# Strassen forms at a different address residue, and the transposed rows as views of one slab, in a two-layer encoder kernel

## The chip, the cores and the metric

The kernel runs on one core of a Trainium2 chip. The metric is the device time of one execution in microseconds; lower is better. TensorE (PE) multiplies; its operands come from the on-chip memory SBUF, where every one of 128 partitions holds the same byte range of a tile, so that a tile has one start address in each partition. Every matmul instruction has two SBUF operands: a stationary one of 128 columns (the "weights", brought in by a weight load that the profile shows on its own row, PEld) and a moving one of up to 512 columns. VectorE (DVE), ScalarE (ACT) and GpSimd (POOL) prepare operands and empty the accumulators; SyncE (SP) issues the DMAs.

## The reference, cut to what matters

Two layers work on one sequence of 512 rows of 1024. Each layer has a mixer (token attention with 12 heads, and attention to 256 memory rows with 4 heads) and a gated feed-forward part with 2816 hidden columns:

```python
h = rms_norm(x, g_mix_pre[i])
proj = h @ w_in[i]
# q, k, v, qm from proj; tok = banded or global attention; mo = memory attention
o = jnp.concatenate([tok, mo], axis=-1) @ w_o[i]
x = x + rms_norm(o, g_mix_post[i])
h = rms_norm(x, g_ffn_pre[i])
gu = h @ w_gate_up[i]
f = (jax.nn.silu(gu[..., :D_FF]) * gu[..., D_FF:]) @ w_down[i]
x = x + rms_norm(f, g_ffn_post[i])
```

## The kernel before

**Numbers in two halves.** A float32 operand is split into a high and a low half of the type fp32r (`split`, lines 284 to 294: ACT writes the high half, DVE the rest). A product is then three matmuls: high by high, high by low, low by high (`mm3`, lines 277 to 281).

**Seven products instead of eight.** In the feed-forward part the 512 tokens are cut into two halves of 256 and the gate and up columns are taken as two halves too; for 20 of the 22 column blocks of a layer a Strassen scheme computes the product by seven products of sums. The sums of the activations are the *forms*: `A11` and `A12` (tile `a1`), `A22` (`a22`), and `nS1`, `S2`, `S3`, `S4` (tile `sf`), each with a high and a low half. They are the moving operands. The sums of the weights (`whi`, `wlo`, tags `hi` and `lo` of the pool `whl`) are the stationary operands. One product is `seven` (lines 1035 to 1043): for each of 4 contraction blocks, three matmuls of 256 columns. One block `f` is thus 7 x 4 x 3 = 84 such matmuls; `body` (from line 1061) runs six of its own products and those of the next block between them, and the preparation of the following weights runs on ACT and DVE beside it. The 20 blocks of a layer go in three lots (6, 6 and 8 blocks), and after each lot the down projection follows (`down`, `down_prod`, 512 moving columns). The first two of the 22 blocks go the plain way (`plain`), with 256 moving columns out of `a1`, `a22` and `a21`.

**Transposed rows.** `hT` holds the transposed, normed rows for the q, k and v products; there it is the stationary operand, and weights of 256 or 384 columns move past it. `th` holds the transposed attention output for the product with `w_o`; it is stationary too, and 512 columns of weights move. In each layer `hT`, `th` and `sf` take turns in the same four places: the pool `hp` has four tiles `h00`, `h01`, `h10`, `h11` of 4 x 512 numbers (8192 bytes in each partition), and a new tile of the same tag waits until every reader of the old one is done.

**Order.** The order of PE's instructions is written out by hand (`manual_schedule`, and the lists of `mixer`); the other engines' order is the tile framework's. A wait is made where an instruction reads or writes a range that an earlier one wrote or read.

**Addresses.** The allocator hands out the tiles of a pool one behind the other; pools of the left side go upward, pools of the right side downward from the top. Nearly all sizes are multiples of 256 bytes, so that the table below gives the remainder of a start address modulo 256, which is what the change moves. Each k-block starts 1024 or 2048 bytes behind the last, so that all parts of a tile share its remainder. In the program before:

| operand | role | layer 0 | layer 1 |
|---|---|---|---|
| `whi`, `wlo` | stationary for forms, moving elsewhere | 192 | 192 |
| `a1`, `a22`, `a21` | moving | 224 | 224 |
| `sf` | moving | 192 | 224 |
| `hT`, `th` | stationary | 192 | 224 |

Of the kernel before, what the change touches and what calls it, by code (L numbers as in the profile page):

```python
# [9 lines left out]
F32 = mybir.dt.float32  # L10
F32R = mybir.dt.float32r
# [5 lines left out]
P = 128  # L17
S = 512
NT = S // P
D = 1024  # L20
KD = D // P
# [17 lines left out]
         (1, 3, LH), (0, 2, HL), (1, 2, HL), (0, 3, HL), (1, 3, HL))  # L39
LATE = {2: 1.2, ("r", 0): 1.05, ("r", 1): 1.3, 3: 2.2, ("r", 2): 2.4, ("r", 3): 3.4, ("m", 0): 4.5, ("m", 1): 5,  # L40
        "rows": 4, ("rm", 0): 6, ("rm", 1): 6.2}
LOTS = ((0, 8), (8, 14), (14, 22))

PACE = [{'lag': 1.692, 'vlag': 0.479, 'jstep': 0.213, 'kstep': 0.375, 'klag': 0.742, 'qoff': [0.212, 0.126, 0.099], 'qlag': 1.02, 'late': 0.6, 'moff': -0.235, 'mdur': 0.562, 'mlag': 0.697, 'kw': [0, 0, 0, 0], 'mw': [2, 1, 1, 0], 'qw': [0, 0, 0, 1, 3, 3, 3, 3], 'hoff': 0, 'ow': [10.3, 10.8, 12.2, 13.2], 'ox': 11.4, 'od': 0.3, 'hstep': 0.872, 'hlag': 1.742, 'hjstep': 0.135, 'hvlag': 0.751, 'owm': [0, 0, 0, 0, 0, 0, 0, 0], 'q0step': 0.27, 'q0off': -0.032, 'q0lag': 0.919, 'm0off': -0.078, 'm0dur': 0.002, 'm0lead': 1.887, 'mlead': 1.201, 'qlead': 0.921, 'q0lead': 1.555, 'qstep': 1.002, 'tw': [0, 0, 0, 0, 0, 0, 0, 0], 'h2off': 0}, {'lag': 1.824, 'vlag': 0.535, 'jstep': 0.218, 'kstep': 0.777, 'klag': 1.715, 'qoff': [-0.027, -0.162, -0.027], 'qlag': 1.189, 'late': 2.15, 'moff': -0.088, 'mdur': 0.384, 'mlag': 1.205, 'kw': [0, 0, 0, 0], 'mw': [0, 0, 0, 0], 'qw': [0, 0, 0, 0, 0, 3, 1, 1], 'hoff': 0, 'ow': [10.2, 10.7, 12.2, 13.2], 'ox': 11.3, 'od': 0.3, 'hstep': 0.946, 'hlag': 1.847, 'hjstep': 0.295, 'hvlag': 0.568, 'owm': [0, 0, 0, 0, 0, 0, 0, 0], 'q0step': 0.718, 'q0off': -0.018, 'q0lag': 1.136, 'm0off': -1.059, 'm0dur': 0.171, 'm0lead': 2.465, 'mlead': 3.162, 'qlead': 1.895, 'q0lead': 1.42, 'qstep': 0.998, 'tw': [0, 0, 0, 0, 0, 0, 0, 0], 'h2off': 0.016}]
# [76 lines left out]
    return bass.AP(tensor=ap.tensor, offset=ap.offset, ap=[[0, P], [1, n]])  # L121


class Forms:

    def __init__(self, trunk, keep, tmp, hp):
        self.tr, self.nc = trunk, trunk.nc
        two = lambda pool, k, tag: [pool.tile([P, k, 256], F32R, tag=f"{tag}{z}", name=tag, bufs=1) for z in range(2)]  # L130
        self.a1, self.a22, self.a21 = two(keep, KD, "a1"), two(keep, 4, "a22"), two(tmp, 4, "a21")
        self.as1 = tmp.tile([P, KD, 256], F32, tag="as1", name="as1", bufs=1)
        self.tmp, self.hp, self.s, self.left = tmp, hp, None, []

    def new_s(self):
        sf = [[self.hp.tile([P, 4, S], F32R, tag=f"h{q}{z}", name="sf", bufs=1) for z in range(2)] for q in range(2)]
        self.s = {n: [sf[i // 2][z][:, :, i % 2 * 256:i % 2 * 256 + 256] for z in range(2)]
                  for i, n in enumerate(("nS1", "S2", "S3", "S4"))}

# [49 lines left out]
class Trunk:  # L189
# [3 lines left out]

    def pool(self, stack, name, side="left", **kw):
        return stack.enter_context(self.tc.tile_pool(name=name, bufs=1, side=side, reuse_waits="tile", **kw))

    def psum(self, stack, name):
        return stack.enter_context(self.tc.tile_pool(name=name, bufs=1, space=bass.MemoryType.PSUM,
                                                      reuse_waits="tile"))
# [169 lines left out]
        return self.tagged(("acc", "acc", "s", "s", "s", "pv")[(self.nbank - 1) % 6])  # L369

    def new_hT(self):
        self.hT = [[self.hp.tile([P, 4, S], F32R, tag=f"h{q}{z}", name="hT", bufs=1) for q in range(2)]
                   for z in range(2)]
        return self.hT

# [428 lines left out]
    def heads_out(self, l, put, xw, xs, x0, dx):  # L804

        self.nbank = 0
        self.wo, self.po, self.th = {}, [], {}
        for u in range(4):
            self.unit(self.a["wo"][l, 0, u], self.side(l, "owm", u), put=put, x=xw[u], dst=self.wo, key=u,
                      pair=("wo", l, 0, u))  # L810

        def part(k):
            if k % 4 == 0:
                self.th[k // 4] = [self.hp.tile([P, 4, S], F32R, tag=f"h{k // 4}{z}", name="th", bufs=1)
                                   for z in range(2)]
            self.split(self.th[k // 4][0][:, k % 4], self.th[k // 4][1][:, k % 4], self.tok[:, k],
                       self.side(l, "tw", k))

        def prod(k, t):
            if t == len(self.po):  # L820
                self.po.append(self.bank())
                if t == 2:
                    self.held = self.turns.pop()
            self.prod(self.po[t], self.heads, KD, k, t, self.wo[k // 2])

        for k in range(KD):
            put(max(xs[k], x0 + (NFILL * k - 1.5) * dx) if k < NH // 2 else xs[k], lambda k=k: part(k))
        for k in range(NH // 2):
            for t in range(NFILL):
                put(max(x0 + (NFILL * k + t) * dx, xs[k] + 0.001 * (t + 1)), lambda k=k, t=t: prod(k, t))  # L830
# [136 lines left out]
    def ffn(self, l, pools, forms, late, done):  # L967
# [156 lines left out]

        for c, (f0, f1) in enumerate(LOTS):
            fs = list(range(f0, f1))
# [22 lines left out]
            for i, f in enumerate(gs):  # L1149
                more = gs[i + 1:] + [None, None]  # L1150
                body(f, f - f0, more[0], more[1], [first, second])
            if c < len(LOTS) - 1:
                self.down(get, self.a["wd"][l], fs, c, o, head)
# [115 lines left out]
    def run(self):  # L1269
        tc, nc, a = self.tc, self.nc, self.a  # L1270
        with ExitStack() as top:
            top.enter_context(tc.manual_schedule(engines={mybir.EngineType.PE}))
            glob = self.glob = self.pool(top, "glob")
            self.small = self.pool(top, "small")
            self.wraw = self.pool(top, "wraw")
            self.whl = self.pool(top, "whl")
            self.ps, self.nbank, self.turns = self.psum(top, "ps"), 0, ["s0", "s1", "s2"]
            dram = self.dram = top.enter_context(tc.tile_pool(name="dram", bufs=1, space=bass.MemoryType.DRAM))
            xs = [[dram.tile([P, D], F32, name=f"x{i}{t}", tag=f"x{i}{t}") for t in range(NT)] for i in range(3)]
            self.spill = dram.tile([P, 2, KD, NMEM], F32, name="smem", tag="smem")  # L1280
            x0 = [a["x"][0, t * P:(t + 1) * P] for t in range(NT)]
            out = [a["out"][0, t * P:(t + 1) * P] for t in range(NT)]

            cst = self.cst = glob.tile([P, 2 * P], F32, name="cst")
            self.ident = cst[:, :P]
            self.ropet = cst[:, P:2 * P].rearrange("p (a t d) -> p a t d", a=2, d=16)
            self.gcol = glob.tile([P, 2, KD], F32, name="gcol")
            self.sink, self.nsink = [glob.tile([P, NH], F32, name=z) for z in ("sink", "nsink")]
            self.gt = glob.tile([P, 2, 2, NT, HD], F32, name="gt")
            self.identr = glob.tile([P, P], F32R, name="identr")  # L1290
            self.mhalf = glob.tile([P, 4], F32, name="mhalf")
            nc.gpsimd.memset(self.mhalf, -0.5)

            hs = [ExitStack() for _ in range(DEPTH + 1)]
            self.hp = self.pool(hs[0], "hT0")
            hb, norm = ExitStack(), ExitStack()
            self.hbuf = self.pool(hb, "h0", side="right")
            self.norm_pool(norm)
            late = {}
            for l in range(DEPTH):  # L1300
                last = l == DEPTH - 1
                mix = ExitStack()
                tokp = self.pool(mix, f"tok{l}")
                core = ExitStack()
                mkp = self.pool(core, f"mk{l}")
                self.mT = tokp.tile([P, 2, KD, NMEM], F32R, tag="tok", name="mT", bufs=1)
                if l == 0:
                    late = self.start(mkp)
                norm.close()
                self.core = self.pool(core, f"core{l}")  # L1310
                self.more = self.core if l else None
                self.mixer(l, mkp, late, tokp)
                self.more = None
                core.close()
                hb.close()

                keep, fts, norm = ExitStack(), ExitStack(), ExitStack()
                forms = Forms(self, self.pool(keep, f"keep{l}", side="right"),
                              self.pool(fts, f"forms{l}", side="right"), self.hp)
                self.norm_pool(norm)  # L1320
                self.hT = None
                late = self.mix_out(l, forms, x0 if l == 0 else xs[1], xs[2 * l])
                mix.close()
                if not last:
                    self.todo = [("wq", 1, c, z) for c in (2, 3) for z in range(2)] + [("wo", 1, 0, u) for u in range(4)]
                ff = ExitStack()
                pools = dict(ff=ff, gu=self.pool(ff, f"gu{l}"), norm=norm, forms=fts)
                get, fs, o, head = self.ffn(l, pools, forms, late, keep.close)
                norm = ExitStack()
                if not last:  # L1330
                    self.hp = self.pool(hs[l + 1], f"hT{l + 1}", side="right")
                    hb = ExitStack()
                    self.hbuf = self.pool(hb, f"h{l + 1}", side="right")
                self.norm_pool(norm)
                late = self.ffn_out(get, a["wd"][l], fs, o, head, a["g_ffn_post"][l], a["g_mix_pre"][1], xs[2 * l], out if last else xs[1], None if last else self.new_rs())
                ff.close()
                if l == 0:
                    hs[0].close()
            norm.close()
            for z in hs[:0:-1]:  # L1340
                z.close()
# [30 lines left out]
```

## Time and profile before

| what | us |
|---|---|
| median of 3 runs (1107.42 to 1108.26) | 1107.56 |
| the profiled execution | 1108.23 |
| its span, first to last instruction | 1106.4 |
| the six runs of `seven` between down projections, 3144 of its 3360 matmuls | 370.4 |
| the rest of the matmul stream and what lies between | 736.0 |

The six runs lie at 221.25 to 276.92, 324.81 to 380.49 and 417.50 to 493.18 us in layer 0, and at 782.85 to 837.45, 885.64 to 940.24 and 977.15 to 1051.35 us in layer 1. Their sum is 55.67 + 55.68 + 75.68 + 54.60 + 54.60 + 74.20. A matmul's row in the timeline has a start that is recorded and an end that is modelled: matmuls follow each other faster than their rows are long. So a matmul's price in a stream is the distance from one start to the next, and where a window holds nothing but matmuls, its length over their number. A window also counts the instruction that began before it and is still open, so that 469 in its row mean 468 starts.

### The profile page before, as it was taken

What the parts mean: (1) busy time and instruction counts of PE and PEld (TensorE: products, weight loads), DVE (VectorE), ACT (ScalarE), POOL (GpSimd) and SP (SyncE); (2) the same over time, 40 slices, a digit from 0 to 9 for tenths busy, and PEclk for the clock granted to TensorE, in tenths of its full rate; (3) what the DMA queues carried; (4) which work ended last, traced back from release to release, by engine and by line L of the source; (5) the groups of instructions that cost most, each with busy time, mean ns of one, the idle gap of its engine ahead of it and who ended that gap; (6) DMA issues with size and microseconds to landing.
All of it is one profiled execution on the core that took longest, in us unless ns stands there. A gap on an engine that the chain in (4) does not pass through costs nothing.

```text
span 1106.4 us, 19515 instructions
## 1 busy us (share of the span) xinstructions
PE 1088.8 (98%) x7436; PEld 1000.2 (90%) x7436; DVE 842.2 (76%) x1433; ACT 659.3 (60%) x1357; POOL 194.9 (18%) x341
## 2 busy tenths in 40 slices
PE   9999999999999999999999999999999999999997
PEld 7899888999889989998898888879998899899986
DVE  7889876999458677875888988758995478668854
ACT  7679975865435535553567888747664365346531
POOL 5773231102000000000444542312000000000001
PEclk9999999999999999999999999999999999999999
DMA  9621017354832562335533221154236133422253
GB/s 335 248 78 39 20 35 252 116 165 133 303 124 86 180 221 78 113 101 190 195 124 115 77 77 39 39 189 154 72 106 207 55 100 115 129 76 97 83 165 115
DMA packets 40702, 142.44 MB, mean 129 GB/s; under 512 B 4768, under 2 KB 5152, under 8 KB 40480
## 3 DMA queue, kind: packets, MB, share of 16 engines
q1 hardware_dynamic: 40320, 140.80, 37.7%
q8 instruction: 58, 0.95, 0.4%
q10 hardware_dynamic: 288, 0.40, 0.1%
q14 instruction: 36, 0.29, 0.1%
HBM read 122.30 MB, written 18.87 MB: 128 GB/s over the span
## 4 chain that ended last, share of the span: by engine, by line
PE 84%; DVE 6%; ACT 4%; POOL 2%; DMA 2%; issue 1%; DVEq 0%; SPq 0%; POOLq 0%; ACTq 0%
PE ps L280 13%; PE ps L279 13%; PE ps L281 13%; PE ps L1043 12%; PE ps L1042 12%; PE ps L1041 12%; PE tp L644 3%; PE o L659 2%; PE o L658 2%; PE s L583 1%; PE s L584 1%; DVE mT L307 1%; ACT whi L289 1%; DVE tl L293 1%; DMA row<-in_x_dram 1%
## 5 line engine op out<-in xcount | busy, mean ns | idle before, releaser
L289 ACT ACTIVATE whi<-raw 128x1024 fp32r<-128x1024 f32 (+3 forms) x206 | 169.2, 839 | 175.9 <-PE ps L1043 73.5
L293 DVE TENSOR_TENSOR wlo<-raw,whi 128x1024 fp32r<-128x1024 f32 (+3 forms) x202 | 191.2, 961 | 74.5 <-ACT whi L289 71.3
L1042 PE MATMUL ps<-sf,wlo 128*128 128x256 f32 x640 | 179.7, 281 | 0.0
L1041 PE MATMUL ps<-sf,whi 128*128 128x256 f32 x640 | 179.7, 281 | 0.0
L1043 PE MATMUL ps<-sf,whi 128*128 128x256 f32 x640 | 179.7, 281 | 0.0
L280 PE MATMUL ps<-wlo,f 128*128 128x512 f32 (+1 forms) x360 | 138.6, 385 | 0.1
L279 PE MATMUL ps<-whi,f 128*128 128x512 f32 (+1 forms) x360 | 138.7, 385 | 0.0
L281 PE MATMUL ps<-whi,f 128*128 128x512 f32 (+1 forms) x360 | 138.4, 384 | 0.0
L1043 PE MATMUL ps<-a,whi 128*128 128x256 f32 x480 | 134.4, 280 | 0.0
L1041 PE MATMUL ps<-a,whi 128*128 128x256 f32 x480 | 134.3, 280 | 0.0
L1042 PE MATMUL ps<-a,wlo 128*128 128x256 f32 x480 | 133.8, 279 | 0.0
L1042 PEld LDWEIGHTS ps<-sf,wlo 128*128 128x128 f32 x640 | 121.4, 190 | 0.5
L1041 PEld LDWEIGHTS ps<-sf,whi 128*128 128x128 f32 x640 | 121.1, 189 | 0.5
L1043 PEld LDWEIGHTS ps<-sf,whi 128*128 128x128 f32 x640 | 121.4, 190 | 0.0
L322 POOL TENSOR_SCALAR e<-sso 128x1 f32<-128x1 f32 x8 | 3.4, 423 | 564.1 <-ACT junk L317 564.0
L634 POOL TENSOR_SCALAR p<-p,rd 128x256 f32<-128x256 f32 (+2 forms) x128 | 76.7, 618 | 101.4 <-DVE rd L631 46.2
L279 PE MATMUL ps<-whi,hT 128*128 128x256 f32 (+1 forms) x304 | 92.6, 305 | 0.0
L1042 PEld LDWEIGHTS ps<-a,wlo 128*128 128x128 f32 x480 | 90.5, 188 | 0.2
L1041 PEld LDWEIGHTS ps<-a,whi 128*128 128x128 f32 x480 | 90.4, 188 | 0.2
L1043 PEld LDWEIGHTS ps<-a,whi 128*128 128x128 f32 x480 | 90.1, 188 | 0.0
L280 PE MATMUL ps<-wlo,hT 128*128 128x256 f32 (+1 forms) x304 | 88.5, 291 | 1.3 <-DVE wlo L293 1.3
L281 PE MATMUL ps<-whi,hT 128*128 128x256 f32 (+1 forms) x304 | 88.2, 290 | 0.0
(207 smaller groups left out, 2703.9 us busy)
## 6 DMA issues: line engine op xcount, KB each, us to landing
raw<-in_wgu_dram SPq DMA_DIRECT2D x48, 512.0 KB, 4.5
raw<-in_wd_dram SPq DMA_DIRECT2D x44, 512.0 KB, 4.4
rb<-in_wgu_dram SPq DMA_DIRECT2D x40, 512.0 KB, 3.6
raw<-in_wo_dram SPq DMA_DIRECT2D x17, 512.0 KB, 4.1
raw<-in_wq_dram SPq DMA_DIRECT2D x16, 512.0 KB, 5.0
xt<-x SPq DMA_DIRECT2D x12, 512.0 KB, 5.2
raw<-in_wm_dram SPq DMA_DIRECT2D x8, 512.0 KB, 4.5
x<-y SPq DMA_DIRECT2D x8, 512.0 KB, 3.1
```

The lines of the kernel that those rows point to most:

```text
L279: mm(out, lh, rh, start=first, stop=False)
L280: mm(out, lh, rl, start=False, stop=False)
L281: mm(out, ll, rh, start=False, stop=last)
L289: a = nc.scalar.activation(hi, src, AF.Copy)
L293: b = nc.vector.tensor_sub(lo, src, hi.bitcast(F32))
L634: self.pooled = nc.gpsimd.tensor_scalar(hd["p"][z][:, :n], hd["p"][z][:, :n], rd[:, z:z + 1], 1.0, op0=OP.mult, op1=OP.mult)
L644: nc.tensor.transpose(tp[:, z], hd["p"][i][:, jj * P:(jj + 1) * P], self.ident)
L658: nc.tensor.matmul(o[:, c0:c1], hd["v"](j), th, start=(j == 0), stop=False, skip_group_check=True)
L659: nc.tensor.matmul(o[:, c0:c1], hd["v"](j), tl, start=False, stop=last, skip_group_check=True)
L1041: mm(out, wh[:, s], rh, start=start and k == 0, stop=False, skip_group_check=True)
L1042: mm(out, wl[:, s], rh, start=False, stop=False, skip_group_check=True)
L1043: mm(out, wh[:, s], rl, start=False, stop=k == 3, skip_group_check=True)
```

## The change

`hp` with its four tiles is replaced by one tile per layer (`hrows`, made by `slab`), and `hT`, `th` and `sf` become views of it at offsets of their own (`rows`; the offsets are in numbers of 4 bytes, in `PLACE`). The forms `a1` and `a22` become views of one tile, `a21` of another, 12 numbers (48 bytes) behind its start (`carve`, `FORM`). Two empty tiles (`gap`) of 224 and 32 bytes move the pools of the right side. No instruction is added or removed in the text of the kernel: splits, matmuls and transfers are the same, with other addresses.

The remainders modulo 256 that follow: in layer 0 the slab starts where `hp` did (192), so `th` (0 numbers) stays at 192, `hT` (22 numbers, 88 bytes) lies at 24 and `sf` (28 numbers, 112 bytes) at 48; the right side starts 224 bytes lower, which is at 0, and `a1`, `a22`, `a21` lie at 48. In layer 1 the gap of 32 bytes and the slab's 48 extra numbers put its start at 0, so `hT` (24 bytes) lies at 24, `th` (192 bytes) at 192, `sf` (48 bytes) at 48, and the forms below it at 48. The weights stay at 192.

| operand | layer 0 before, after | layer 1 before, after |
|---|---|---|
| `a1`, `a22`, `a21` | 224, 48 | 224, 48 |
| `sf` | 192, 48 | 224, 48 |
| `hT` | 192, 24 | 224, 24 |
| `th` | 192, 192 | 224, 192 |

```diff
+FORM = 12
+PLACE = (128, dict(hT=22, th=0, sf=28)), (48, dict(hT=6, th=48, sf=FORM))
...
+def carve(pool, name, ks):
+
+    t = pool.tile([P, 256 * sum(ks) + 64], F32R, tag=name, name=name, bufs=1)
+    cut = [(FORM + 256 * sum(ks[:i]), 256 * k) for i, k in enumerate(ks)]
+    v = [t[:, a:a + n].rearrange("p (k n) -> p k n", n=256) for a, n in cut]
+    return [v[i:i + 2] for i in range(0, len(v), 2)]
...
-        two = lambda pool, k, tag: [pool.tile([P, k, 256], F32R, tag=f"{tag}{z}", name=tag, bufs=1) for z in range(2)]
-        self.a1, self.a22, self.a21 = two(keep, KD, "a1"), two(keep, 4, "a22"), two(tmp, 4, "a21")
+        self.a1, self.a22 = carve(keep, "a1", [KD, KD, 4, 4])
+        (self.a21,) = carve(tmp, "a21", [4, 4])
...
-        sf = [[self.hp.tile([P, 4, S], F32R, tag=f"h{q}{z}", name="sf", bufs=1) for z in range(2)] for q in range(2)]
+        sf = [[self.tr.rows(q, z, "sf") for z in range(2)] for q in range(2)]
...
+    def gap(self, stack, name, n):
+
+        self.pool(stack, name, side="right").tile([P, n], F32, name="gap", bufs=1)
+
+    def slab(self, stack, l, **kw):
+
+        room, self.place = PLACE[l]
+        self.hrows = self.pool(stack, f"hT{l}", **kw).tile([P, 16 * S + room], F32R, name="hrows", bufs=1)
+
+    def rows(self, q, z, name):
+
+        a = self.place[name] + (2 * q + z) * 4 * S
+        return self.hrows[:, a:a + 4 * S].rearrange("p (k n) -> p k n", n=S)
...
-        self.hT = [[self.hp.tile([P, 4, S], F32R, tag=f"h{q}{z}", name="hT", bufs=1) for q in range(2)]
+        self.hT = [[self.rows(q, z, "hT") for q in range(2)]
                    for z in range(2)]
...
-                self.th[k // 4] = [self.hp.tile([P, 4, S], F32R, tag=f"h{k // 4}{z}", name="th", bufs=1)
+                self.th[k // 4] = [self.rows(k // 4, z, "th")
                                    for z in range(2)]
...
-            self.hp = self.pool(hs[0], "hT0")
+            self.slab(hs[0], 0)
...
+                if l == 0:
+                    self.gap(keep, "gap0", 56)
                 forms = Forms(self, self.pool(keep, f"keep{l}", side="right"),
-                              self.pool(fts, f"forms{l}", side="right"), self.hp)
+                              self.pool(fts, f"forms{l}", side="right"))
...
-                    self.hp = self.pool(hs[l + 1], f"hT{l + 1}", side="right")
+                    self.gap(hs[l + 1], "gap1", 8)
+                    self.slab(hs[l + 1], 1, side="right")
```

## What was predicted

> **What bounds the kernel now.** I read the page first, then PE's waits, then the matmul stream stage by stage, because the change touches nothing but addresses and can act on time only through instructions that read or write the moved tiles.
>
> ```profile
> span 1106.4 us, 19515 instructions
> PE 1088.8 (98%) x7436; PEld 1000.2 (90%) x7436; DVE 842.2 (76%) x1433; ACT 659.3 (60%) x1357; POOL 194.9 (18%) x341
> PEclk9999999999999999999999999999999999999999
> PE 84%; DVE 6%; ACT 4%; POOL 2%; DMA 2%; issue 1%; DVEq 0%; SPq 0%; POOLq 0%; ACTq 0%
> L1041 PE MATMUL ps<-sf,whi 128*128 128x256 f32 x640 | 179.7, 281 | 0.0
> L1041 PE MATMUL ps<-a,whi 128*128 128x256 f32 x480 | 134.3, 280 | 0.0
> ...
> PE tp L644 <- DVE tl L293: 2.6, 7, 0.7
> PE o L658 <- DVE tok L667: 2.4, 5, 0.7
> ```
>
> PE holds 84% of the chain that ended last, at the full clock in every slice, and its longest waits sum to a few microseconds in the whole span. Lines 1041, 1042 and 1043 each have 640 + 480 = 1120 instructions, so the forms' products are 3360 matmuls. Nothing before them was idle (the last column is 0.0), so their time is not waiting; it is the distance from one start to the next. The windows that hold only them show it:
>
> ```profile
> 324.81:380.49 55.68, 55.68 (x469) 1.00 0.32 107
> 417.50:493.18 75.68, 75.68 (x637) 1.00 0.30 96
> 885.64:940.24 54.60, 54.60 (x469) 1.00 0.33 108
> 977.15:1051.35 74.20, 74.20 (x637) 1.00 0.30 97
> ```
>
> Layer 0: 55.68/468 = 119.0 ns and 75.68/636 = 119.0 ns. Layer 1: 54.60/468 = 116.67 and 74.20/636 = 116.67. The same instructions, shapes and clock, and no wait: 2.3 ns differ. What differs in the code's terms is the form's remainder minus the weight's, modulo 256, which I call the offset. In layer 0 `sf` stands at offset 192 - 192 = 0 and the `a` forms at 32; in layer 1 all stand at 32. One product on `sf` (12 matmuls) in each layer, first and next start:
>
> ```profile
> 441.74 0.28 PE L1041 MATMUL ps<-sf,whi 128*128 128x256 f32 x1
> 441.86 0.28 PE L1042 MATMUL ps<-sf,wlo 128*128 128x256 f32 x1
> ...
> 443.18 0.28 PE L1041 MATMUL ps<-a,whi 128*128 128x256 f32 x1
> ...
> 999.90 0.28 PE L1041 MATMUL ps<-sf,whi 128*128 128x256 f32 x1
> 1000.02 0.28 PE L1042 MATMUL ps<-sf,wlo 128*128 128x256 f32 x1
> ...
> 1001.30 0.28 PE L1041 MATMUL ps<-sf,whi 128*128 128x256 f32 x1
> ```
>
> 1.44/12 = 120.0 ns at offset 0, 1.40/12 = 116.67 at 32. So PE's stream bounds the kernel, and the address has a price in it already. How much of a matmul is not streaming? Other streams without waits answer it:
>
> ```profile
> 22.87:24.78 1.91, 1.91 (x13) 1.00 1.02 392
> 27.03:29.67 2.64, 2.64 (x24) 1.00 0.77 271
> 163.28:189.17 25.89, 25.89 (x115) 1.00 0.76 263
> 569.79:573.00 3.21, 3.21 (x29) 1.00 0.50 158
> 724.31:750.90 26.59, 26.59 (x115) 1.00 0.62 219
> ```
>
> These have `hT` or `th` as stationary operand. Each count is one or two above the starts in the window. At offset 0 (layer 0): 384 columns 1.91/11 = 173.6 ns, 256 columns 2.64/22 = 120.0, 512 columns 25.89/114 = 227.1. From 256 to 512 columns that is 107.1/256 = 0.418 ns a column; 256 columns stream in 107 ns, and a **remainder** of 13 ns is left, the same at every length. At offset 32 it is 116.67 - 107 = 9.7. At offset 224, that is -32 (layer 1): 3.21/27 = 118.9, remainder 11.9; 26.59/114 = 233.2, remainder 19.2.
>
> **The change part by part.**
>
> *Forms to offset 112.* After the change every form lies at 48, the weights at 192: 48 - 192 = -144, or 112. No row of this trace has that offset, nor any start at an odd multiple of 16, so its remainder is bounded by the nearest rows: from nothing (107 ns) to the largest seen, 19.2 (126 ns). Between them there is a trend: 19.2 or 11.9 at -32, 13 at 0, 9.7 at 32. It looks like two readers of one memory, the moving stream and the next weight load, which collide less the further ahead one is. A straight line, 3.3 less for each 32 bytes, comes to 13 - 3.5 x 3.3 = 1.5 at 112. Nothing shows that it goes on so far. I take the middle between the nearest row (9.7) and the line's end (1.5): a remainder of 5.6, and so 112.6 ns. Layer 0: 1680 x (119.0 - 112.6) = 10.8 us. Layer 1: 1680 x (116.67 - 112.6) = 6.8 us. Together -17.6.
>
> [...]
>
> *The plain blocks.* 2 blocks x 2 x 2 halves x 8 x 3 = 192 matmuls a layer read `a1`, `a22`, `a21`:
>
> ```profile
> 207.16:221.25 14.09, 14.09 (x124) 1.00 0.14 41
> 768.76:782.85 14.09, 14.09 (x124) 1.00 0.12 38
> ```
>
> 120 of them take 14.09/120 = 117.4 ns (the rest of the count belongs to instructions open at the edges and transposes). 384 x (117.4 - 112.6) = -1.8 us.
>
> *`th` in layer 1 goes from offset -32 to 0.* 114 matmuls in one stage change from 233.2 to the 227.1 of layer 0: -0.7 us. In layer 0 `th` stays.
>
> *`hT` goes to 24, offset 168.* 960 matmuls (2 layers x (4 x 32 + 32) x 3). Their starts are not multiples of 16, which no row shows either. [...] Bounds: remainder 8 gives 960 x 4.5 = -4.3; 19.2 gives 960 x 6.8 = +6.5.
>
> *Waits.* One slab instead of four tiles: a view overlaps the row of the neighbour by up to 168 bytes. `th` row k is written after the q products have read all of `hT`, by the order in `heads_out`, and `sf` only after the plain blocks of the next part have begun; the old tags had the same order. A false wait would hold one split of DVE or ACT, and PE does not stand behind one in the waits above. Cost 0; one late split, if it came, costs about 0.7 us, as PE's longest waits do.
>
> *What is late next.* DVE prepares the weights beside PE, and its slack decides what PE can keep:
>
> ```profile
> 444.75 1.23 DVE L293 TENSOR_TENSOR wlo<-ru,whi 128x1024 fp32r<-128x1024 f32 x1 [0.90 <-ACT whi L289]
> 448.75 1.23 DVE L293 TENSOR_TENSOR wlo<-raw,whi 128x1024 fp32r<-128x1024 f32 x1 [0.30 <-ACT whi L289]
> ...
> 221.25:276.90 55.65, 55.65 (x470) 55.65 (x469) 53.05 (x75) 32.93 (x57) 6.32 (x7) 1.00 0.47 150
> 782.85:837.45 54.60, 54.60 (x471) 54.60 (x469) 50.93 (x75) 32.92 (x57) 0.00 (x0) 1.00 0.34 108
> ```
>
> A block of 84 matmuls lasts 84 x 119.0 = 10.0 us, and in the one from 439.9 to 449.9 DVE's only idle times are the 0.90 + 0.30 in brackets: 8.8 us of work against 84 x 112.6 = 9.5. It fits. The tightest place is the first lot of layer 0, where DVE (the third busy column, after PE and PEld) works 53.05 of 55.65 us: PE at 112.6 would need 52.7, so 0.4 us may come back as waiting.
>
> Sum: -17.6 - 1.8 - 0.7 + 0 + 0.4 = -19.7. The profiled execution took 1108.2, of which 1.8 lie outside its span; the median shown is 0.7 lower. 1108.2 - 19.7 = 1088.5, on the median's footing **1088**.
>
> **The rivals.**
> *As at 32.* The remainder settles at 9.7, because the collisions come in fixed steps and odd 16 adds nothing: 1680 x 2.3 + 384 x 0.7 + 0.7 = -4.9, **1102.7**. For it: two streams (L1 forms) sit at exactly 116.67 for hundreds of matmuls.
> *The line holds.* Remainder 1.5, 108.5 ns: 1680 x 10.5 + 1680 x 8.2 = 31.4, plain 3.4, `th` 0.7; DVE gives back 53.05 - 468 x 0.1085 = 2.3 in the first lot: -33.2, **1074**. For it: three offsets in order. Against: the jump to 19.2 at -32 is no straight line.
> *A worse lock: slower.* A start in the middle of a 32-byte step lets the two readers meet again at every step, as at offset 0: 120.0 in both layers. 1680 x 1.0 + 1680 x 3.33 + 384 x 2.6 - 0.7 = +7.6, **1115**. It is slower as soon as the forms' mean remainder passes today's 10.8 ns (119.0 and 116.67 averaged, less 107). For it: the locks depend on address in a way that I read from three points.
> *No effect.* The remainder does not follow the offset but the layer (its other tiles differ too), or the remainders are not reached: **1107.6**. Against it stand `sf` and `a` within layer 0: 119.0 on average while `sf` alone takes 120.0. [...]
>
> **How the numbers follow.** Forecast 0.36, as at 32 0.20, the line 0.20, slower 0.19, no effect 0.05. A measurement here tells 0.2%, some 2.2 us, from no change. Faster: 0.36 + 0.20 + most of 0.20 (`hT`'s +6.5 can eat the 4.9) = 0.73; same: 0.08; slower: 0.19. The forecast's own range is 1080 to 1096. For 8 in 10 the range reaches to the line's case and cuts what lies below it, and into the slower case: 1071 to 1113.
>
> **What would show it.** The windows of the forms' products: length over starts near 112.6 in both layers and equal, not 119.0 and 116.67; starts on `sf` and on `a` alike. 116.67 in both is the second case, under 110 the third, 120 the fourth. The stage of `th` in layer 1: 227 ns a matmul. The windows of `hT`: still 119 to 120. PE's waits: DVE's weight splits in the first lot of layer 0 appear if PE outruns DVE; a wait of ACT or DVE on PE's reads of `hrows` would show a false dependency. The forecast is wrong if the remainder at 112 is not on the slope between 32 and the line's end.

## The result, and the profile after

| | before | after |
|---|---|---|
| median (four runs of each, on one chip) | 1107.49 us | 1097.35 us (1097.01 to 1097.84) |
| ratio of after to before, 95% interval | | 0.9907 [0.989, 0.9925] |
| the profiled execution, its span | 1108.23, 1106.4 us | 1097.01, 1094.9 us |
| forecast, range | | 1088, 1071 to 1113 |

The change takes 10 us of the 20 that were forecast. The page after, its busy times, the chain that ended last and the groups of the forms' products (lines are those of the kernel after; 1041 has become 1065, 293 has become 317):

```profile
span 1094.9 us, 19518 instructions
...
PE 1072.8 (98%) x7436; PEld 985.0 (90%) x7436; DVE 840.8 (77%) x1433; ACT 659.1 (60%) x1357; POOL 197.7 (18%) x341
...
PE 70%; DVE 5%; issue 2%; ACT 1%; POOL 1%; DMA 0%; DVEq 0%; POOLq 0%; ACTq 0%
...
L1065 PE MATMUL ps<-hrows,whi 128*128 128x256 f32 x640 | 176.2, 275 | 0.0
...
L1065 PE MATMUL ps<-a,whi 128*128 128x256 f32 x480 | 132.3, 276 | 2.9 <-DVE c L1101 2.9
```

PE still sets the end: it is busy for 98% of the span. (The shares of its chain sum to 79% only, so the 70% of PE is no sign of a new bound.) One thing is new in the last row: 2.9 us of waiting ahead of products on `a`, where there was 0.0. The windows of the six lots of `seven` show start and end, length, the busy time of PE, PEld, DVE, ACT and POOL, each with its number of instructions, then the granted clock, the busy share of the DMA engines and their GB/s:

```profile
222.00:277.67 55.67, 53.40 (x471) 53.20 (x469) 52.88 (x76) 33.08 (x58) 7.13 (x7) 1.00 0.45 148
325.44:378.52 53.08, 53.08 (x470) 53.08 (x468) 43.69 (x64) 32.81 (x56) 0.00 (x0) 1.00 0.33 110
415.39:487.50 72.11, 72.11 (x637) 72.11 (x636) 61.90 (x91) 44.76 (x75) 0.00 (x0) 1.00 0.30 99
775.94:830.20 54.26, 53.59 (x470) 53.29 (x469) 51.32 (x76) 33.05 (x58) 0.00 (x0) 1.00 0.33 107
878.01:931.09 53.08, 53.08 (x469) 53.07 (x468) 43.62 (x64) 33.05 (x56) 0.00 (x0) 1.00 0.34 110
967.97:1040.09 72.12, 72.12 (x637) 72.11 (x636) 61.91 (x91) 44.76 (x75) 0.00 (x0) 1.00 0.30 99
```

The second and third lot of each layer hold 468 and 636 matmuls: 53.08/468 = 72.12/636 = 113.4 ns in both layers, where layer 0 had 119.0 and layer 1 116.67. The first lots do not follow. That of layer 0 lasts 55.67 us as before, though PE is busy for 53.40 of it only, and that of layer 1 lasts 54.26 where 53.08 would do. The windows of the plain blocks in both layers, and that of `th` in layer 1 (PE alone in the last row):

```profile
208.25:221.99 13.74, 13.74 (x123) 13.74 (x122) 13.74 (x23) 11.13 (x18) 0.00 (x0) 1.00 0.13 42
762.20:775.94 13.74, 13.74 (x123) 13.74 (x122) 13.74 (x23) 11.17 (x18) 0.00 (x0) 1.00 0.13 39
718.21:744.07 25.86, 25.86 (x116) 1.00 0.61 222
```

Stage by stage (length after less length before, both in the profiled executions):

| stage | us |
|---|---|
| lots of layer 0: first, second, third | 0.00, -2.60, -3.56 |
| lots of layer 1: first, second, third | -0.33, -1.52, -2.08 |
| plain blocks, the two windows | -0.70 |
| `th` in layer 1 | -0.73 |
| mixer of layer 0 (16 to 163 us) | +1.30 |
| mixer of layer 1 | -0.33 |
| everything else | -1.0 |
| span | -11.5 |

So three questions are open: why the distance is 113.4 at this offset, what holds the first lots, and what the mixer of layer 0 lost. The waits of PE after (microseconds in total, times, the longest) point at places for the last two:

```profile
PE tp L668 <- DVE tl L317: 3.1, 7, 1.4
PE ps L1065 <- DVE c L1101: 2.9, 2, 2.3
```

### The profile page after: what moved, and what is told of

It is laid out like the page before. It is cut to its first block, busy times and chain, and to the rows that moved or that the text cites. A ratio compares the mean times of both kernels' runs of the same rounds, so it can differ in the third digit from the quotient of the medians.

```text
span 1094.9 us, 19518 instructions
## 1 busy us (share of the span) xinstructions
PE 1072.8 (98%) x7436; PEld 985.0 (90%) x7436; DVE 840.8 (77%) x1433; ACT 659.1 (60%) x1357; POOL 197.7 (18%) x341
## 4 chain that ended last, share of the span: by engine, by line
PE 70%; DVE 5%; issue 2%; ACT 1%; POOL 1%; DMA 0%; DVEq 0%; POOLq 0%; ACTq 0%
PE ps L1065 11%; PE ps L1066 11%; PE ps L1067 11%; PE ps L304 10%; PE ps L303 10%; PE ps L305 10%; PE tp L668 2%; DVE wlo L317 1%; PE o L683 1%; PE o L682 1%; PE s L607 1%; PE s L608 1%; POOL r L337 1%; DVE hrows L317 1%; POOL p L658 0%
## 5 line engine op out<-in xcount | busy, mean ns | idle before, releaser
L1066 PE MATMUL ps<-hrows,wlo 128*128 128x256 f32 x640 | 176.4, 276 | 0.0
L1065 PE MATMUL ps<-hrows,whi 128*128 128x256 f32 x640 | 176.2, 275 | 0.0
L1067 PE MATMUL ps<-hrows,whi 128*128 128x256 f32 x640 | 176.2, 275 | 0.0
L303 PE MATMUL ps<-whi,hrows 128*128 128x256 f32 (+2 forms) x432 | 144.1, 333 | 0.0
L304 PE MATMUL ps<-wlo,hrows 128*128 128x256 f32 (+2 forms) x432 | 138.0, 320 | 1.6 <-DVE wlo L317 1.6
L305 PE MATMUL ps<-whi,hrows 128*128 128x256 f32 (+2 forms) x432 | 138.0, 320 | 0.0
L1065 PE MATMUL ps<-a,whi 128*128 128x256 f32 x480 | 132.3, 276 | 2.9 <-DVE c L1101 2.9
L1067 PE MATMUL ps<-a,whi 128*128 128x256 f32 x480 | 132.1, 275 | 0.0
L1066 PEld LDWEIGHTS ps<-hrows,wlo 128*128 128x128 f32 x640 | 120.1, 188 | 0.6
L1065 PEld LDWEIGHTS ps<-hrows,whi 128*128 128x128 f32 x640 | 120.1, 188 | 0.5
L1067 PEld LDWEIGHTS ps<-hrows,whi 128*128 128x128 f32 x640 | 120.1, 188 | 0.0
```

What stands on the lines that cost most here:

```text
L303: mm(out, lh, rh, start=first, stop=False)
L304: mm(out, lh, rl, start=False, stop=False)
L305: mm(out, ll, rh, start=False, stop=last)
L1065: mm(out, wh[:, s], rh, start=start and k == 0, stop=False, skip_group_check=True)
L1066: mm(out, wl[:, s], rh, start=False, stop=False, skip_group_check=True)
L1067: mm(out, wh[:, s], rl, start=False, stop=k == 3, skip_group_check=True)
```

## The experiments

"Offset" is, as above, the start of the moving form less the start of the weight, modulo 256. Ratios are to the kernel before on the same chip; a time without a ratio is that of one execution.

### Addresses apart from views

e1 keeps the views and puts every address back:

```diff
-FORM = 12
-PLACE = (128, dict(hT=22, th=0, sf=28)), (48, dict(hT=6, th=48, sf=FORM))
+FORM = 0
+PLACE = (0, dict(hT=0, th=0, sf=0)), (0, dict(hT=0, th=0, sf=0))
...
-    t = pool.tile([P, 256 * sum(ks) + 64], F32R, tag=name, name=name, bufs=1)
+    t = pool.tile([P, 256 * sum(ks)], F32R, tag=name, name=name, bufs=1)
...
-                if l == 0:
-                    self.gap(keep, "gap0", 56)
...
-                    self.gap(hs[l + 1], "gap1", 8)
```

> The views of one slab and of two form tiles, with the start addresses of before (weights 192; forms 224 and 192 in layer 0, 224 in layer 1; transposed rows as before). Theory A (addresses make the gain, the slab's finer waits let the splits of the attention output go earlier on ACT and DVE and delay PE at 124 to 134 us of layer 0): no gain, 119.0 and 116.67 ns a forms' matmul as before, and 1.5 to 2 us slower than before: 1109.2. Rival B (the views themselves gain something, or the mixer's loss comes from the shifted hT): 1107.5 or less, PE's mixer of layer 0 as before.

Measured: 1109.08 us, ratio 1.0013 [1.0003, 1.0022]. The windows of the second lots of both layers:

```profile
326.20:381.88 55.68, 55.68 (x469) 1.00 0.31 106
886.75:941.35 54.60, 54.60 (x470) 1.00 0.33 109
```

55.68/468 = 119.0 and 54.60/468 = 116.67, the distances of before. All that was gained is in the addresses, and e1 takes 1.4 us more than before: the mixer of layer 0 is 1.6 us longer than before here too. The next run shows what that is.

e2 does the reverse: addresses of after, but four tiles again in layer 0, each 256 bytes longer so that the rows can lie at their own places (layer 1 keeps the slab, for want of room):

```diff
+        if self.hp:
+            t, a = self.hp.tile([P, 4 * S + 64], F32R, tag=f"h{q}{z}", name=name, bufs=1), self.place[name]
+            return t[:, a:a + 4 * S].rearrange("p (k n) -> p k n", n=S)
         a = self.place[name] + (2 * q + z) * 4 * S
```

> The addresses of the changed kernel, but layer 0's transposed rows in four tiles with tags, as before, each 256 bytes longer. Theory A: the mixer of layer 0 gets its order on ACT and DVE back and some 1.7 us with it: 1095.6, with 113.4 ns in the forms' products. Rival B: no gain over the changed kernel, 1097.4, the loss at 124 to 134 us stays, because it comes from hT's new address.

Measured: 1095.43 us (1094.23 to 1097.24), ratio 0.9891 [0.9876, 0.9906]. The mixer of layer 0 is 146.9 us long (after 148.5, before 147.2), and its longest wait, in the row that stood at 1.4 after, is 0.7 again:

```profile
PE tp L672 <- DVE tl L321: 2.3, 7, 0.7
PE ps L1069 <- DVE c L1105: 2.2, 2, 1.6
```

With the slab, the first of DVE's two splits of `th` runs 0.9 us earlier in the row of instructions (0.47 us behind the split of `q` ahead of it, in e2 1.38 us), and a second weight split (`wlo`, 0.68 us) stands ahead of the `tl` on which PE waits at 130 us. With four tiles the old order is back. So views of one tile in place of tiles of their own change the order of DVE's instructions, and with it the wait of 0.7 us becomes one of 1.4.

That wait is not what the mixer lost. All eleven traces with the order of after have it, and in nine of them the mixer lasts 147.0 to 147.6 us, about as long as before. Only after and e1 are longer, and there the granted clock fell within 0.8 us behind the wait. The same instructions, from the first behind that wait on, in after, e1, e7 (an experiment below, with the same wait) and before (PE's busy time, granted clock, DMA share, GB/s):

```profile
130.55:135.61 5.06, 5.06 (x21) 0.66 0.32 104
130.75:135.82 5.07, 5.07 (x21) 0.66 0.34 103
130.62:134.11 3.49, 3.49 (x22) 1.00 0.39 150
130.70:134.19 3.49, 3.49 (x22) 1.00 0.00 0
```

For 3.4 us of this stretch (130.6 to 134.0 us in after, 131.5 to 134.9 in e1) the granted clock was 0.5, and the same work took 1.57 us longer: all of the 1.3 us. What brings the drop into one execution and not into another, no run shows; that nine traces with the same wait are without it leaves open whether the order has a part in it. The times of e1 fit: its five executions with a mean granted clock of 0.998 or 0.999 took 1107.90 to 1109.01 us (the middle one 1108.48), the five with 0.997 or 0.996 took 1109.14 to 1110.82. So the views without the drop cost some 0.8 us by the medians, and the rest of the 1.4 goes with the clock.

### `hT` back to offset 0

```diff
-PLACE = (128, dict(hT=22, th=0, sf=28)), (48, dict(hT=6, th=48, sf=FORM))
+PLACE = (128, dict(hT=0, th=0, sf=28)), (48, dict(hT=48, th=48, sf=FORM))
```

> Only hT goes back to a start at 192 (offset 0), the rest as in the changed kernel. If offset 168 made its matmuls cheaper (256 columns 116.6 ns in the changed kernel against 119.4 and 118.3 before), some 700 such matmuls lose about 2 ns each: 1.5 us slower than the changed kernel, 1098.9. If PE stands behind other engines in the mixer anyhow: the same time, 1097.4, though the matmuls without waits read 120 ns again.

Measured: 1095.8 us, ratio 0.99 [0.9883, 0.9917], not slower than after. The mixer of layer 1 lasts 0.4 us longer; in layer 0 the clock stays at 1.00, and the mixer lasts 147.3 us. `hT` at offset 168 has 116.6 ns a matmul after (mean over 606 distances; those over 129 ns, which are waits, are left out) where it had 119.0 and 118.3 before, but in the mixer PE waits for others so often that little of it arrives.

### Is it DVE's amount of work that holds the first lots?

In the first lots DVE is busy for nearly the whole time (52.88 of 55.67 us). e4 moves two of its differences, in `finish`, to GpSimd:

```diff
-                v.tensor_sub(s1, a22, a21)
+                self.nc.gpsimd.tensor_tensor(s1, a22, a21, op=OP.subtract)
...
-                v.tensor_sub(s3, self.as1[:, :4, c], a21)
+                self.nc.gpsimd.tensor_tensor(s3, self.as1[:, :4, c], a21, op=OP.subtract)
```

> Two of the subtractions per token block that make the sums of the activations (s1 and s3 of finish, four per layer, 0.6 us each on DVE) run on GpSimd. Theory: DVE bounds the first lot of each layer, so the 2.2 us wait of layer 0 shrinks by about the 2.4 us taken off DVE, and layer 1's 0.6 us goes: 1097.4 - 2.8 = 1094.6. Rival: the chain through GpSimd (slower per instruction) delays the first forms as much, or PE waits elsewhere: 1097 or more.

Measured: 1107.71 us, ratio 0.9994 [0.9985, 1.0004]. It lost all that the change had gained; the first lots last 58.29 and 59.24 us, and the plain blocks 2.1 us more in each layer. Its first row of waits, and the two lots:

```profile
PE ps L1065 <- ACT p L1071: 6.5, 2, 3.3
```

```profile
223.11:281.40 58.29, 55.02 (x471) 54.83 (x469) 53.39 (x76) 35.19 (x59) 6.35 (x7) 0.97 0.42 141
781.76:841.00 59.24, 55.98 (x471) 55.78 (x469) 51.67 (x76) 35.46 (x59) 0.00 (x0) 0.94 0.29 99
```

The differences feed each other and then the splits of `sf`; on GpSimd the two took 2.3 and 1.5 us on the mean in layer 0, where DVE needs 0.7 each, and the whole chain came later. Each lot has one wait of 3.3 us, and in it or shortly behind it the granted clock fell to 0.5, for 3.4 us in layer 0 and for 6.8 in layer 1 (0.97 and 0.94 on the mean of the lot). As a test of DVE's load it is spoilt. e7 takes work away instead, and leaves part of the computation out, the third sum of weights in the blocks of the first lots:

```diff
         def prep_d(f):
-            nc.vector.tensor_add(raw[f][:, 512:], raw[f][:, 512:], st[f]["ru"][:, 512:])
+            if f >= 8:
+                nc.vector.tensor_add(raw[f][:, 512:], raw[f][:, 512:], st[f]["ru"][:, 512:])
```

> The third sum of weights (line 1056, the second half of raw plus ru) is left out for the blocks of the first lot of each layer, so their products with A22 use the raw half alone: about 6 x 0.7 us of DVE's work less in each first lot. If DVE sets the length of the first lots (theory D), the wait of 2.3 us in the first lot of layer 0 and of 0.7 in layer 1 goes, PE runs at its distance of 113.4 and both lots come to 53.1 to 53.3: 2.5 and 1.1 us less, 1093.8. If the wait comes from the order of the instructions or from ACT (rival), the lots keep 55.7 and 54.3 and the time stays at 1097.

Measured: 1095.58 us. The first lots of layers 0 and 1, and the sums `ru<-raw,rb` of DVE in the second of them:

```profile
220.63:275.42 54.79, 53.67 (x470) 53.28 (x469) 49.28 (x70) 33.45 (x58) 6.89 (x7) 1.00 0.44 150
773.65:828.24 54.59, 53.42 (x471) 53.23 (x469) 47.99 (x70) 33.57 (x58) 0.00 (x0) 1.00 0.31 107
```

```profile
L1043 DVE TENSOR_TENSOR ru<-raw,rb 128x512 f32<-128x512 f32 x5 | 3.4, 689 | 1.6 <-DMA rb<-in_wgu_dram 1.6
```

DVE has 3.6 and 3.3 us less to do, but the lots come to 54.79 (from 55.67) and 54.59 (from 54.26), not to 53.1. So the amount of work alone is not the bound. What is new in layer 1 is that DVE stands idle for a DMA of `rb`. Looked for in the kernel after, the same stands there in layer 0 (start, length, engine, line, and in brackets the idle time before and who ended it):

```profile
236.32 1.22 DVE L317 TENSOR_TENSOR wlo<-rb,whi 128x1024 fp32r<-128x1024 f32 x1
...
237.56 0.33 SPq L1041 DMA_DIRECT2D rb<-in_wgu_dram  x1
...
242.66 0.69 DVE L1043 TENSOR_TENSOR ru<-raw,rb 128x512 f32<-128x512 f32 x1 [1.39 <-DMA rb<-in_wgu_dram]
243.28 1.22 DVE L317 TENSOR_TENSOR wlo<-ru,whi 128x1024 fp32r<-128x1024 f32 x1
244.41 0.42 DVE L1101 TENSOR_TENSOR c<-ps,p 128x256 f32<-128x256 f32 x1
...
244.88 0.39 PE L1065 MATMUL ps<-a,whi 128*128 128x256 f32 x1 [2.27 <-DVE c L1101]
```

Read from the top: the split of one block ends at 237.54 and frees a buffer of `rb`; the load of a later block into it is issued 0.02 us afterwards; its data let DVE go on at 242.66, and until then DVE stands idle for 1.39 us, though the operands of `c`, two places further on, are there (the last matmul into the bank that it reads started at 239.62). PE may not write the bank before `c` has read it, and waits 2.27 us. The same sums in the same lot of the kernel before:

```profile
L1019 DVE TENSOR_TENSOR ru<-raw,rb 128x512 f32<-128x512 f32 x5 | 3.4, 689 | 0.5 <-issue 0.3 <-DMA rb<-in_wgu_dram 0.2
```

There DVE stood 0.2 us for that DMA, and PE, at 119.0 ns a matmul, waited for nothing in the lot. So a queue is likely: a sum that is not ready stands ahead of one that is. e11 tests it, on top of e2:

```diff
+        sum5 = None
...
-            with self.tc.issue_after(forms.last[1]) if f == 3 else nullcontext():
+            after = forms.last[1] if f == 3 else sum5 if (l, f) == (0, 5) else None
+            with self.tc.issue_after(after) if after else nullcontext():
...
-            nc.vector.tensor_add(c[:, 256:], x, d["p5"])
+            nonlocal sum5
+            sum5 = nc.vector.tensor_add(c[:, 256:], x, d["p5"]).ins
```

> e2 (the addresses of after, four tiles again in layer 0) with one order more: the first sum of weights of block 5 in layer 0 (ru<-raw,rb) is issued behind the sum c of block 3. In the first lot of layer 0 of after and of e2, DVE stands 0.8 to 1.4 us idle before that sum, for the DMA of rb, whose buffer came free late; c, whose operands are there, stands behind it, and PE waits 2.3 us (1.6 in e2) for c before it may write the bank again. Theory Q (a queue: the wait of PE is DVE's order behind a DMA): the wait of 1.6 us falls to 0.3 or less (one split of 1.2 us still stands before c), the lot comes to 53.5 to 53.8 us instead of 55.0 and the time to 1094.1. Theory C (capacity: DVE's 53 us of work in this lot are the bound, whatever the order): the wait comes back at another place of the lot, which keeps 54.7 to 55.0, and the time stays at 1095.4.

Measured: 1094.13 us (1093.31 to 1094.56), ratio 0.988 [0.9863, 0.9896]. The first lot of layer 0, and the row of waits that stood at 2.2 in e2:

```profile
220.40:274.43 54.03, 53.36 (x471) 53.17 (x469) 53.05 (x76) 32.69 (x58) 6.12 (x7) 1.00 0.47 153
```

```profile
PE ps L1072 <- DVE c L1109: 1.2, 2, 0.7
```

And DVE around `c` in its timeline:

```profile
240.01 1.23 DVE L321 TENSOR_TENSOR wlo<-ru,whi 128x1024 fp32r<-128x1024 f32 x1 [0.41 <-ACT whi L317]
241.16 0.42 DVE L1109 TENSOR_TENSOR c<-ps,p 128x256 f32<-128x256 f32 x1
241.49 0.68 DVE L1050 TENSOR_TENSOR ru<-raw,rb 128x512 f32<-128x512 f32 x1
```

The sum now follows `c`, without a wait for the DMA. The lot falls from 55.01 to 54.03 us, and the wait in it from 1.6 to 0.7. DVE is as busy as ever: 53.05 of 54.03. The queue was the larger part, as theory Q has it, but 0.7 us stay where 0.3 at most was expected, and the lot misses the 53.5 to 53.8 expected: a weight split of 1.23 us still stands ahead of `c` and waits 0.41 us for ACT. With 53.05 us of DVE's work in a lot that PE could do in 53.08, any idle time of DVE can now reach PE. Against e2 the medians differ by 1.3 us but the intervals of the ratios overlap; that e11 is faster than after (1093.31 to 1094.56 against 1097.01 to 1097.84) is clear of the spread. It beats both kernels.

### What is special about 112?

The forecast had read a slope from three offsets. e5 and e6 give each of four groups of forms an offset of its own, with `FORM` made to depend on the layer, and move `hT` and `th` too:

```diff
-FORM = 12
-PLACE = (128, dict(hT=22, th=0, sf=28)), (48, dict(hT=6, th=48, sf=FORM))
+FORM = (0, 16)
+PLACE = (128, dict(hT=36, th=0, sf=24)), (48, dict(hT=28, th=48, sf=4))
```

> Distances between starts (ns a matmul of 256 columns) by offset (start of the moving form minus start of the weight, modulo 256). Layer 0: a forms at 64, sf at 96; layer 1: a forms at 128, sf at 80; hT of layer 0 at 112 with the roles swapped (the weights move, hT stands), hT of layer 1 at 80. Theory S (3.3 ns less for each 32 bytes, down to a floor of 113.3): 113.4 at 64, 113.3 at 80, 96 and 128; hT 113.3 to 114 in both layers instead of 116.6, because only the difference counts. Theory O (only odd multiples of 16 are good): 113.3 at 80 and at 112, 116.7 at 64, 96 and 128, so that layer 0's forms cost 116.7 as layer 1's did before (the time 1680 x 3.4 = 5.7 us more than after's in layer 0 and about half of that in layer 1: 1105). By S the time is after's less up to 960 x 2.5 = 2.4 us for hT: 1095 to 1097. Theory A (the absolute address of the form counts, not the difference): hT stays at 116.6 or more whatever its offset.

```diff
+FORM = (52, 24)
+PLACE = (128, dict(hT=40, th=36, sf=36)), (48, dict(hT=16, th=20, sf=14))
```

> The same with other offsets. Layer 0: a forms at 16, sf at 144; layer 1: a forms at 160, sf at 120 (half of an odd multiple of 16); hT of layer 0 at 96, of layer 1 at 128; th at 112 in both layers, with 512 columns. Theory S: 118.4 at 16, 113.3 at 120, 144 and 160, hT 113.3 to 114, th 113.3 + 106.9 = 220.2 instead of 227. Theory O: 113.3 at 16 and 144, 116.7 at 160, hT 116.7. Where the collision is periodic in 128 bytes instead of 256 (theory P), 144 costs what 16 costs and 160 what 32 costs, 116.7, and hT at 128 costs 120. Time by S: after's 1097.3 with a loss of 720 x 5.1 = 3.7 us for the a forms of layer 0 and a gain of 228 x 6.8 = 1.6 for th and 2.4 for hT: 1097; by P about 1103.

Measured: 1112.76 and 1111.87 us, slower than before. Theories S and O fail, and P does not fit at 160; theory A is left to e10 below. The mean distances between starts (some 900 in each group, by the tile that is read; distances over 129 ns, which are waits, are left out) are 117.3 at 16, 117.7 at 64, 119.2 at 80, 119.9 at 96, 120.5 at 120, 119.6 at 128, 117.8 at 144 and 118.2 at 160. There is no slope to a floor, nor are the odd multiples of 16 better. A mixture in one layer might itself do harm: in before, `a` at offset 32 took 118.1 ns on the mean in layer 0, beside `sf` at 0, and 116.7 in layer 1, where all stood at 32. So e8 and e9 give all forms of a layer one offset: 80 and 176, then 48 and 208.

> In e5 and e6 the a forms and sf lay at different offsets and every stream was slow (117.3 to 120.5 ns), at 80 and 144 too. Here all forms of a layer share one offset: 80 in layer 0 (start 16), 176 in layer 1 (start 112); hT starts at 48 in layer 0 and at 176 in layer 1. Theory O (odd multiples of 16 are good, a mixture of offsets is not): 113.4 ns a matmul in both layers and the time of after, 1097. Theory U (one particular place is good, and the neighbours 96, 80, 128 are not): 117 to 120 in layer 0 at 80 as in e5, so windows of 54.8 to 56 us for 468 matmuls; 176 then says whether there is a second place. Time by U: 1680 x 4 to 6 us a layer, 1104 to 1112.

> The two odd multiples of 16 on the other side: all forms at offset 48 in layer 0 (start 240), at 208 in layer 1 (start 144); hT starts at 240 and 160. Theory O: 113.4 in both. Theory U: 116.7 to 120 in both, since 32 cost 116.67 and 64 cost 117.7. A middle case: 48 on the way from 32 (116.67), between 113.4 and 116.7. Times: 1097 by O, 1104 to 1112 by U.

Measured: 1114.54 and 1111.38 us. The second lots of layers 0 and 1, of e8 and then of e9:

```profile
325.34:381.49 56.15, 56.15 (x470) 1.00 0.30 105
888.82:944.63 55.81, 55.81 (x470) 1.00 0.32 106
```

```profile
325.03:380.42 55.39, 55.39 (x469) 1.00 0.32 105
885.78:941.54 55.76, 55.76 (x469) 1.00 0.33 107
```

Over 468 starts these are 120.0 ns at 80, 119.3 at 176, 118.4 at 48 and 119.1 at 208. The mixture was not the reason at 80, and 112 stays alone, as theory U has it. Then the difference against the address itself: e10 moves the weights by 32 bytes.

```diff
+            self.pool(top, "gapw").tile([P, 8], F32, name="gap", bufs=1)
             self.whl = self.pool(top, "whl")
...
+FORM = (12, 20)
+PLACE = (120, dict(hT=14, th=56, sf=20)), (48, dict(hT=6, th=48, sf=20))
```

> The weights are moved by 32 bytes, to 224 (a gap of 8 numbers ahead of their pool; the slab of layer 0 gives up 8 numbers, so that the rest stays). Layer 0: forms start at 48 as in after, and their offset to the weights is 80. Layer 1: forms start at 80, so the offset is 112 as in after. Theory D (the difference of form and weight decides): layer 0 as 80 in e5 and e8, 117 to 120; layer 1 113.4. Theory A (the start of the moving form decides): layer 0 113.4, layer 1 117 to 120. If neither layer has 113.4, both starts count (theory B). The rest of the stream changes too (weights at 224 against f, hT and th), so the total says little: 1097 to 1112.

Measured: 1109.09 us. The second lot of layer 0 (forms where after has them, offset 80) and the third of layer 1 (forms at another place, offset 112):

```profile
327.33:383.48 56.15, 56.15 (x470) 1.00 0.31 106
980.32:1052.44 72.12, 72.12 (x638) 1.00 0.30 99
```

56.15/468 = 120.0 and 72.12/636 = 113.4: the same two values as at 80 in e8 and at 112 in after, to the hundredth of a microsecond. The difference decides, and not the address of the form (48 in the one window, as in after) or of the weight (224 in both). Last, one number (4 bytes) to either side, with `FORM = (11, 13)`:

> All forms one number to either side: offset 108 in layer 0 (start 44), 116 in layer 1 (start 52). Until here 0, 16, 32, 48, 64, 80, 96, 120, 128, 144, 160, 176 and 208 cost 116.7 to 120.5 ns a matmul and 112 alone 113.4. Theory N (112 is a point: only starts at a whole multiple of 16 bytes fall into this rhythm): 117 to 120 in both layers, windows of 54.8 to 56.2 us for 468 matmuls, 1108 to 1113 in all. Theory W (a window some bytes wide, where the next weight load's reads fall between those of the moving operand): 113.4 to 114 in at least one of the two, 1097 if in both.

Measured: 1118.87 us. The second lots, offset 108 and offset 116:

```profile
325.81:381.96 56.15, 56.15 (x469) 1.00 0.32 105
890.30:947.24 56.94, 56.94 (x469) 1.00 0.33 104
```

56.15/468 = 120.0 and 56.94/468 = 121.7, the worst of all. 112 is a point and no window.

## Why the prediction was right, and where not

Its direction and its range were right, with the time 9 us above the forecast and above the 1080 to 1096 that it calls the forecast's own range. By its own steps:

**What bounds the kernel.** Right: PE's stream, with a price in the address. e1 has the distances of before with the new views, and e10 shows that the offset to the weight is the right quantity. The "no effect" rival is out: the same matmuls cost 113.4 ns at 112 (after), 120.0 at 80 (e8, e10) and 121.7 at 116 (e12).

**Forms to offset 112, 112.6 ns.** The number was nearly right (113.4) and the reason wrong. The step that failed is "a straight line, 3.3 less for each 32 bytes". The two readers that collide were the author's guess at its cause; the runs show distances by offset, and not what makes them. At 48, 64, 80 and 96, which lie on that line, the runs showed 118.4, 117.7, 120.0 and 119.9 (64 and 96 in a mixture), all above the 116.67 at 32. Four bytes beside the chosen place stands 121.7. That the middle between a row and the line's end came out 0.8 ns from the measurement was luck. Had the starts been laid 4 bytes off, the rival "a worse lock" would have come true, with more than its 1115 us; the forecast itself had noted for that rival that the locks depend on the address "in a way that I read from three points". Its reason, a start in the middle of a 32-byte step, does not hold: 80 and 112 are both such starts, at 120.0 and 113.4 ns. In size the 0.8 ns cost 3360 x 0.8 = 2.7 us.

**The plain blocks.** 13.74/120 = 114.5 ns instead of 112.6: 0.7 us seen in the two windows, of 1.8 forecast.

**`th` in layer 1.** Right: 25.86/114 = 226.8 ns, 0.73 us gained.

**`hT`, counted as 0.** No run shows the 0, an estimate of the author: at offset 168 the distance improved (116.6 against an unchanged 119 to 120), which e3 shows to be worth about 0.4 us in layer 1 and nothing that can be told in layer 0.

**Waits of the views, cost 0.** Nearly right in size, and incomplete. The forecast looked for a false wait and found none, rightly; it did not see that views in place of tiles also change the order in which DVE's instructions are laid out. That made a wait of 0.7 us one of 1.4, yet left the mixer of e7 as long as before (147.2 us); by the medians of e1 it costs some 0.8 us, about the one late split that the forecast had priced at 0.7. The 1.3 us that the mixer of after lost, and that the sum has no term for, are the 3.4 us at half the granted clock.

**What is late next.** The place was named (DVE in the first lot of layer 0), the price was not: 0.4 us against 2.6 us there, and nothing against 1.2 us in layer 1. The step compared DVE's busy time with PE's need, 53.05 with 52.7, as if DVE would never stand still. But here DVE stood 1.39 us for a late load while a sum further down its list was ready. It is mis-sized in the sum and wrong in kind: e7 took over 3 us of work from DVE with little effect, and one changed place in the order (e11) gave 1.0 us.

Between the sum of -19.7 and the -11.5 of the spans lie 8.2 us: 2.7 for the distance, 2.2 + 1.2 for the first lots, 1.1 for the plain blocks (1.8 less the 0.7 seen) and 1.3 for the mixer of layer 0, less 0.3 that the mixer of layer 1 gained, make 8.2.

## What to carry to other kernels

When a stream of matmuls without waits shows different distances at different addresses, the offset between its two operands is a parameter to be swept in steps of a few bytes, since three points do not make a slope and 4 bytes cost 6.6 ns of 113.4. Before counting the gain of a faster engine, follow the order of the engine that feeds it to the first instruction that can be late; busy time alone does not show it (one changed place in DVE's order gave 1.0 us here, over 3 us less work 0.9 at most). Views cut from one tile in place of separate tiles may change other engines' order (here a wait of 0.7 us became 1.4), so try the address and the view apart. Where a stage changes its length by more than its waits do, read the granted clock of that stretch: two traces of the same program order differed by 1.57 us in 3.49 by that alone.

## What the runs showed of the hardware

Distances from start to start of matmuls with 256 moving columns, forms moving, one offset in the layer (0 alone is read from `sf` beside `a` at 32; one product gave 120.0, the mean of all 960 is 119.6):

| offset | 0 | 32 | 48 | 80 | 108 | 112 | 116 | 176 | 208 |
|---|---|---|---|---|---|---|---|---|---|
| ns | 120.0 | 116.7 | 118.4 | 120.0 | 120.0 | 113.4 | 121.7 | 119.3 | 119.1 |
| run | before (`sf`) | before | e9 | e8, e10 | e12 | after, e10 | e12 | e8 | e9 |

In two other streams 112 was not the good offset. With 512 columns, `th` at offset 112 cost 26.6 us for its 114 matmuls in e6 where offset 0 cost 25.9, and the weights moved past `hT` at 112 took 118.9 ns in e5, more than the 116.6 at 168. That the offset counts modulo 256 is taken over from the prediction; no run was made for the period. Why 112 is the point for the forms was not found; nor were the offsets from 224 up to 252 tried for them, nor a single offset for a whole layer at 16, 64, 96, 120, 128, 144 and 160. Most of the 64 offsets in steps of 4 bytes were tried nowhere, so that a better one may exist.

The granted clock was 1.00 in the windows of these distances. It fell to 0.5 for 3.4 us in the mixers of after and e1, within 0.8 us behind a wait of PE of 1.4 us, and for 3.4 and 6.8 us in the first lots of e4, in a wait of 3.3 us or within 1.2 us behind it; nine other traces had the wait of 1.4 us and kept 1.00.
